# Two-chunk down products for both blocks of the paired FFN, with moved casts, moved sums of squares and an out-projection operand written by attention

## The chip, the cores and the metric

One core of a Trainium2 chip runs the kernel. The metric is the device time of one execution in microseconds (us). Below, PE is the matrix engine, DVE the vector engine, ACT the scalar engine, POOL GpSimd, and SP the engine whose queue issues nearly all DMAs. A *wait* is the time in which an engine's next instruction stands ready in its order but something that it needs is not done.

## The reference

All arrays are fp32: `x_sample` is 512 tokens, `x_prompt` 1024, of 1024 channels. Two layers run over both groups: layer 0 mixes tokens by a grouped Fourier transform, layer 1 by attention, and each is followed by a SwiGLU feed-forward network (FFN) with 2816 hidden channels.

```python
def attention_mixer(x, g, w_qkv, q_gain, k_gain, w_o, cos, sin):
    h = rms_norm(x, g)
    qkv = h @ w_qkv
    q, k, v = jnp.split(qkv, [Q_DIM, Q_DIM + KV_DIM], axis=-1)
    ...
    sc = jnp.einsum('bqkgd,bskd->bkgqs', qi, k).astype(jnp.float32) * scale
    p = jax.nn.softmax(sc, axis=-1).astype(v.dtype)
    return jnp.einsum('bkgqs,bskd->bqkgd', p, v)
    ...
    return o @ w_o

def swiglu_ffn(x, g, w_gate, w_up, w_down):
    h = rms_norm(x, g)
    return (jax.nn.silu(h @ w_gate) * (h @ w_up)) @ w_down

x = x + fourier_mixer(...) or attention_mixer(...)
x = x + swiglu_ffn(x, norm_ffn[i], ffn_w_gate[i], ffn_w_up[i], ffn_w_down[i])
```

There are 8 query heads and 2 key/value heads of 128, with RMS norm and rotary positions on queries and keys.

## The kernel before

**Tiles.** The tokens are three blocks of 512: block 0 is the sample, blocks 1 and 2 the prompt. Channels lie on the 128 partitions, so a block is 8 tiles of 128x512, and its residual lies in DRAM (`xres`). The hidden channels are 22 chunks of 128. Every product is made of three matmuls (`mm3`, lines 255 to 257): each operand is split into a high part in the matrix engine's format, which ACT casts (L248 for activations, L293 for weights), and a low part, the difference, which DVE or POOL subtracts (L249, L294).

**The single FFN** (`ffn`, block 0 of either layer) goes chunk by chunk: gate products `g` (24 matmuls), up products, SiLU, product, split into a `mid` tile, and then the down products `c`, 8 output tiles, which DVE adds to accumulators (L780). The down products of earlier chunks are put as items between later gate and up products (`one()`).

**The paired FFN** (`ffn_pair`, blocks 1 and 2) computes gate and up of two chunks for two blocks with seven matrix products in place of eight. Its steps are named by their moving operands, B11, B21, T2, T1, B22, T3, N4. Each step runs four j, 2 x 3 matmuls for each. The operands are sums and differences of the four normed quarters of the two blocks; `moving` computes them once per layer, writes them to DRAM, and `fetch` brings them back as pieces of 128x1024 fp32 into a ring of eight slots. In layer 1 some operands (`places`) stay in SBUF after their first load. A chunk's down weights are loaded and cast by `fetch_down`, called in the middle of B21 and T3. The down products of a block wait in the list `pend`, and `some()` takes from it between the ring matmuls. There are 11 iterations of two chunks.

**Order.** `weave` interleaves two generators by their stated costs, a main one (F) and a second (X); inside, each engine's instructions keep an order that the Tile scheduler chose, and each engine executes its own in order. The main stages in time: the sample's Fourier mixer (to about 195 us); the single FFN of layer 0 woven with the prompt's mixer and then `moving` (to about 540); pair 0, the paired FFN of layer 0, woven with block 0's attention (to about 1420); the single FFN of layer 1 woven with the prompt's projections, attention (1750 to 2150), out-projection and `moving` (to about 2340); pair 1, alone on PE, to the end.

**Around the change.** `new_residual` takes a block's output tiles one by one, stores them, and adds their squares (ACT L344, DVE L345); with the last one `rstd_cols` sums over the partitions by four small matmuls (L314) and runs a DVE chain. `attend` computes for each head and query tile the scores, their maximum (L1194), its product with the query's norm (L1195), the exponentials `p` (L1198), transposes, and the values; the output goes to DRAM (`dot`), and `reloaded` brings it back as the operand of the out-projection, for each block.

Of the kernel before, what the change touches and what calls it, by code (L numbers as in the profile page):

```python
# [17 lines left out]
P = 128  # L18
D = 1024
# [106 lines left out]
def trunk_kernel(ctx: ExitStack, tc: tile.TileContext, t: dict):  # L126
# [18 lines left out]
    for name, kw in (("sbH", {}), ("sbF", {}), ("sbX", {}), ("psF", PS), ("psX", PS)):  # L145
# [186 lines left out]
    def new_residual(b, dc, piece, out=None, stays=False, room=None):  # L332
# [6 lines left out]
        if dc == 0:  # L339
            ss[b] = room() if room else tl("ss", [TB], F32, "ss" + cur[0])  # L340
# [5 lines left out]
        if dc == NC - 1:  # L346
            rstd[b] = cp.tile([P, 4], F32, name=nm("rs"))
            rstd_cols(rstd[b], ss.pop(b), D)

    def normed(b, gain, got, ab, held=None):  # L350

        yield 2.0
# [404 lines left out]
    def ffn(layer, b, h, out=None):  # L757
# [52 lines left out]
        for fc in range(NF):  # L810
# [6 lines left out]
            for dc in range(NC):  # L817
# [5 lines left out]
                if not odd_ and dc >= 3:  # L823
                    one()
                if dc % 2:
                    yield 1.36 if odd_ or dc < 3 else 2.0 if dc == 3 else 2.7
# [3 lines left out]
            for dc in range(NC):  # L830
                if not odd_ and dc == 1:
                    want("gate", fc + 1)
                if dc == (2 if odd_ else 4):
                    want("up", fc + 1)
                if not (here and fc == 0):
                    part(wu, h, up, dc)
                if not odd_:
                    one(2 if dc == 3 else 1)
                elif dc >= 6:
                    one()  # L840
                if dc % 2:
                    yield 3.4 if not odd_ and dc == 3 else 2.7 if not odd_ or dc == 7 else 1.36
# [22 lines left out]
    def moving(blocks, gain, out, ring, helped):  # L865

        yield 2.0
        r = [in_rows(rstd[b]) for b in blocks]
        yield 1.0
        for j in range(4):  # L870
# [7 lines left out]
            for (d, k), x in v.items():  # L878
                dve.scalar_tensor_tensor(x, x, gain[:, 4 * d + j : 4 * d + j + 1], r[k], op0=ALU.mult, op1=ALU.mult)  # L879
# [19 lines left out]
            dve.tensor_tensor(v[0, 0], v[0, 1], v[0, 0], op=ALU.subtract)  # L899
            put("T1", v[0, 0])  # L900
# [3 lines left out]
            dve.tensor_tensor(v[1, 1], v[1, 1], v[0, 0], op=ALU.subtract)  # L904
# [3 lines left out]
            yield 5.0  # L908

    def ffn_pair(layer, blocks, ring, places, wide, outs):  # L910
# [5 lines left out]
        pieces, turns = [ring[:, n] for n in range(8)], [0]  # L916
        del order[:8]

        def fetch():
            if order:  # L920
                v, j = order.pop(0)
# [4 lines left out]
                else:  # L926
                    x = ring[:, turns[0] % 8]
                    turns[0] += 1
                sp.dma_start(x.bitcast(F32), mov[layer][v][:, j])
# [3 lines left out]
        first_raw = acc_tile("raw", [2, TB], F32)  # L933
        for b in blocks:
            accs[b] = kept[b] = accumulators()

# [4 lines left out]

        def down(b, parts, dc, begins, ends):
# [562 lines left out]
```

## Time and profile before

| quantity | value |
|---|---|
| median of three runs | 3043.49 us (3035.97 to 3046.52) |
| the profiled execution | 3038.65 us |
| its span | 3036.9 us |
| PE busy | 2925.5 us, 96% |
| POOL busy | 1338.7 us, 44% |
| DVE busy | 1487.2 us, 49% |
| DMA, mean | 180 GB/s |
| PE's granted clock, mean | 0.985 |

In the profile `L954` is a line of the kernel before; `acc<-c,acc` gives what is written and read, by the program's names without numbers; `x368` is a count. A view of windows gives, for a stretch of time, the busy time of each engine with its instructions, then the mean clock that PE was granted (PEclk, 1 is full), the share of the DMA engines' time and their rate. A PE busy share of 1 at a clock of 1 is the most that a stretch can do.

### The profile page before, as it was taken

What the parts mean: (1) busy time and instruction counts of PE and PEld (TensorE: products, weight loads), DVE (VectorE), ACT (ScalarE), POOL (GpSimd) and SP (SyncE); (2) the same over time, 40 slices, a digit from 0 to 9 for tenths busy, and PEclk for the clock granted to TensorE, in tenths of its full rate; (3) what the DMA queues carried; (4) which work ended last, traced back from release to release, by engine and by line L of the source; (5) the groups of instructions that cost most, each with busy time, mean ns of one, the idle gap of its engine ahead of it and who ended that gap; (6) DMA issues with size and microseconds to landing.
All of it is one profiled execution on the core that took longest, in us unless ns stands there. A gap on an engine that the chain in (4) does not pass through costs nothing. (4 is left out here: it accounts for less than half of the span.)

```text
span 3036.9 us, 37132 instructions
## 1 busy us (share of the span) xinstructions
PE 2925.5 (96%) x13920; PEld 2407.4 (79%) x13920; DVE 1487.2 (49%) x2537; ACT 1235.8 (41%) x1931; POOL 1338.7 (44%) x746
## 2 busy tenths in 40 slices
PE   7999989999999999999999999999998999999999
PEld 6888867778888788887778787788776788888887
DVE  6664663544436554336543456555335344444444
ACT  6543332333326664223444476777433222222221
POOL 4444345445444446542443322221546654555462
PEclk9999999999999999999999999999998999999999
DMA  7435474877767778865533211121657954445342
GB/s 228 153 118 174 167 259 134 289 273 241 248 228 250 238 232 290 298 229 191 187 121 102 90 60 59 60 67 46 207 178 256 332 194 154 139 153 198 134 139 90
DMA packets 204212, 547.15 MB, mean 180 GB/s; under 512 B 22304, under 2 KB 36640, under 8 KB 203648
## 3 DMA queue, kind: packets, MB, share of 16 engines
q1 hardware_dynamic: 203104, 539.99, 52.7%
q0 software_dynamic: 640, 3.74, 0.4%
q8 instruction: 109, 1.79, 0.2%
q10 hardware_dynamic: 288, 1.05, 0.1%
q14 instruction: 71, 0.58, 0.1%
HBM read 472.34 MB, written 72.35 MB: 179 GB/s over the span
## 5 line engine op out<-in xcount | busy, mean ns | idle before, releaser
L294 POOL TENSOR_TENSOR w<-raw,w 128x1024 fp32r<-128x1024 f32 x244 | 589.0, 2421 | 921.9 <-ACT w L293 898.3
L249 POOL TENSOR_TENSOR w<-raw,w 128x512 fp32r<-128x512 f32 (+1 forms) x332 | 436.9, 1337 | 620.1 <-ACT w L248 597.6
L954 DVE TENSOR_TENSOR acc<-c,acc 128x512 f32<-128x512 f32 x368 | 253.1, 689 | 410.7 <-PE c L257 402.9
L255 PE MATMUL c<-mid,w 128*128 128x512 f32 x1056 | 418.8, 397 | 20.5 <-ACT mid L248 9.0
L257 PE MATMUL c<-mid,w 128*128 128x512 f32 x1056 | 416.0, 394 | 4.0 <-POOL w L294 4.0
L256 PE MATMUL c<-mid,w 128*128 128x512 f32 x1056 | 416.2, 394 | 3.6 <-DVE mid L249 3.5
L293 ACT CAST w<-raw 128x1024 fp32r<-128x1024 f32 x244 | 254.9, 1049 | 319.0 <-PE c L257 111.4
L248 ACT CAST w<-raw 128x512 fp32r<-128x512 f32 (+1 forms) x332 | 197.2, 635 | 442.1 <-issue 185.7
L255 PE MATMUL g<-h,w 128*128 128x512 f32 x704 | 284.0, 403 | 7.6 <-ACT w L293 4.9
L257 PE MATMUL g<-h,w 128*128 128x512 f32 x704 | 281.7, 400 | 3.8 <-POOL w L294 3.8
L256 PE MATMUL g<-h,w 128*128 128x512 f32 x704 | 281.8, 400 | 0.0
L255 PEld LDWEIGHTS c<-mid,w 128*128 128x128 f32 x1056 | 199.9, 189 | 72.5 <-ACT mid L248 13.5
L257 PEld LDWEIGHTS c<-mid,w 128*128 128x128 f32 x1056 | 200.1, 190 | 47.4 <-POOL w L294 6.4
L256 PEld LDWEIGHTS c<-mid,w 128*128 128x128 f32 x1056 | 200.0, 189 | 47.4 <-DVE mid L249 7.7
L256 PE MATMUL c<-h,w 128*128 128x512 f32 x480 | 190.1, 396 | 7.7 <-POOL h L249 5.4
L255 PE MATMUL a<-ring,w 128*128 128x512 f32 x488 | 193.6, 397 | 3.5 <-DVE x L879 3.5
L257 PE MATMUL a<-ring,w 128*128 128x512 f32 x488 | 191.8, 393 | 3.0 <-POOL w L249 3.0
L255 PE MATMUL c<-h,w 128*128 128x512 f32 x480 | 190.5, 398 | 2.3 <-ACT h L248 1.4
L256 PE MATMUL a<-ring,w 128*128 128x512 f32 x488 | 191.7, 393 | 0.0
L257 PE MATMUL c<-h,w 128*128 128x512 f32 x480 | 188.3, 393 | 0.0
L780 DVE TENSOR_TENSOR acc<-c,acc 128x512 f32<-128x512 f32 x176 | 120.5, 687 | 130.8 <-PE c L257 128.5
L255 PEld LDWEIGHTS g<-h,w 128*128 128x128 f32 x704 | 135.9, 193 | 36.5 <-ACT w L293 6.0
(368 smaller groups left out, 5948.9 us busy)
## 6 DMA issues: line engine op xcount, KB each, us to landing
ring<-mov_B SPq DMA_DIRECT2D x204, 512.0 KB, 6.0
ring<-mov_T SPq DMA_DIRECT2D x176, 512.0 KB, 4.8
raw<-in_gate_dram SPq DMA_DIRECT2D x44, 512.0 KB, 3.6
raw<-in_up_dram SPq DMA_DIRECT2D x44, 512.0 KB, 3.6
raw<-in_down_dram SPq DMA_DIRECT2D x88, 256.0 KB, 3.1
raw<-in_gate_dram SPq DMA_DIRECT2D x88, 256.0 KB, 3.2
raw<-in_up_dram SPq DMA_DIRECT2D x88, 256.0 KB, 4.8
raw<-in_down_dram SPq DMA_DIRECT2D x44, 512.0 KB, 5.2
```

Source lines behind the costliest of these rows:

```text
L248: act.copy(hi, src)
L249: eng.tensor_tensor(lo, src, hi.bitcast(F32), op=ALU.subtract)
L255: pe.matmul(out, lh, rh, start=first, stop=False)
L256: pe.matmul(out, lh, rl, start=False, stop=False)
L257: pe.matmul(out, ll, rh, start=False, stop=last)
L293: pinned(act.copy(flat[:, 0], raw)) if early else act.copy(flat[:, 0], raw)
L294: pool.tensor_tensor(flat[:, 1], raw, flat[:, 0].bitcast(F32), op=ALU.subtract)
L780: dve.tensor_tensor(acc[dc], box[0], acc[dc], op=ALU.add)
L954: dve.tensor_tensor(acc, box[0], acc, op=ALU.add)
```

## The change

- *moving*: of the four normed quarters at every j, two are written to PSUM (`bank2`); the differences are ordered so that each reads one of them. The tiles of B22 and T3 get a pool of their own (three buffers). POOL makes the low parts of B21, T1, T3 and N4 in both layers; before, of B11 and B21 in layer 0, of B11, B21, B22, T3 and N4 in layer 1.
- *single FFN*: in the gate products the down items begin with weight tile 5 instead of 3, and three tiles of the up products take two items; the next gate weights are asked for two tiles later.
- *paired FFN*: the down products of both blocks are done after N4's beginning, two chunks at once for each (before, block 1's first chunk went alone in the first iteration, the last alone at the end). The products lie in four fixed slots, one of which is the eighth slot of the ring, so the ring of operands has seven. The down weights are loaded at the first j of T1 and of B22 and cast at the first j of B22 and T3. In layer 1 two quarters of gate and up weights are loaded one step earlier, in a pool of six.
- *end of pair 0*: the sums of squares get one tile a block, and the matmuls L314 with the chain behind them are made where the norm is first used (`settled`). The projections of layer 1 begin with block 2.
- *attention*: the maximum is taken bank by bank, and maximum and product are one instruction. For block 0, and for block 1 of the prompt, the values go straight into the operand of the out-projection (`straight`); for block 2 the way through DRAM stays.

```diff
 def normed(b, gain, got, ab, held=None):
+    settled(b)
 ...
 def ffn(layer, b, h, out=None):
-                if not odd_ and dc >= 3:
+                if not odd_ and dc >= 5:
                     one()
...
-                if not odd_ and dc == 1:
+                if not odd_ and dc == 3:
                     want("gate", fc + 1)
+                if fc == NF - 1 and dc == 4:
+                    want("B", f0)
...
-                    one(2 if dc == 3 else 1)
+                    one(2 if dc in (2, 4, 6) else 1)
 def moving(...):
+            a2 = bank2()
+            for (d, k), x in list(v.items()):
+                if d == k:
+                    v[d, k] = a2[:, d]
+                dve.scalar_tensor_tensor(v[d, k], x, gain[...], r[k], op0=ALU.mult, op1=ALU.mult)
...
+                elif name in ("B22", "T3"):
+                    x = tl("l", [2, TB], F32R, "mv", staging)
...
-            dve.tensor_tensor(v[0, 0], v[0, 1], v[0, 0], op=ALU.subtract)
-            put("T1", v[0, 0])
+            t1 = x4[:, 0, 0]
+            dve.tensor_tensor(t1, v[0, 1], v[0, 0], op=ALU.subtract)
+            put("T1", t1)
 def ffn_pair(...):
+        def load_down(fc):
+            coming[fc] = raw_tile(D)
+            sp.dma_start(coming[fc], t["down"][layer, fc])
+        def fetch_down(fc):
+            wds[fc] = w_tile(2, NC, P)
+            flat = wds[fc].rearrange("p h c n -> p h (c n)")
+            split(flat[:, 0], flat[:, 1], coming.pop(fc), eng=pool)
...
+        slots = [two[0], two[1], tl("mid", [2, TB], F32R, "m2", raws), ring[:, 7]]
+        where = {(0, 0): (0, 1), (0, 1): (1, 0), (1, 1): (2, 2), (1, 0): (3, 3)}
...
-            for i, ps in (yield from step("B21", lambda: fetch_down(f0), 2)):
+            for i, ps in (yield from step("B21")):
-            for i, ps in (yield from step("T2", lambda: downs(blocks[0], begins=f0 == 0), 2)):
+            for i, ps in (yield from step("T2")):
-            for i, ps in (yield from step("T1")):
+            for i, ps in (yield from step("T1", lambda: load_down(f0), 0)):
-            for i, ps in (yield from step("B22")):
+            for i, ps in (yield from step("B22", lambda: (fetch_down(f0), load_down(f1)), 0)):
-            for i, ps in (yield from step("T3", lambda: fetch_down(f1), 2)):
+            for i, ps in (yield from step("T3", lambda: fetch_down(f1), 0)):
-            for i, ps in (yield from step("N4", lambda: downs(blocks[1], begins=f0 == 0, ends=f0 + 2 == NF), 0)):
+            for i, ps in (yield from step("N4", lambda: downs(blocks[1], f0), 1)):
...
-        downs(blocks[0], ends=True)
+            downs(blocks[0], f0)
 def attend(blocks, straight, slot):
-                    dve.tensor_reduce(st[:, 0:1], s_in, op=ALU.max, axis=AX.X)
-                    dve.tensor_tensor(st[:, 1:2], st[:, 0:1], nrqc[:, gq, h : h + 1], op=ALU.mult)
+                    for kb in range(nb):
+                        dve.tensor_reduce(st[:, 2 * kb : 2 * kb + 1], sc[:, kb], op=ALU.max, axis=AX.X)
+                    dve.scalar_tensor_tensor(st[:, 1:2], st[:, 2 * nb - 2 : 2 * nb - 1], st[:, 0:1], nrqc[:, gq, h : h + 1], op0=ALU.max, op1=ALU.mult)
...
+                    if blocks[n] == straight:
+                        split(hs[:, 0, h, c0 : c0 + 256], hs[:, 1, h, c0 : c0 + 256], po[:, 0:256])
+                        return
 def aux_1():
-        yield from attend((0,))
+        yield from attend((0,), 0, "A")
 def aux_2():
-        for b in (1, 2):
+        for b in (2, 1):
             yield from qkv(b, kept[b])
-        yield from attend((1, 2))
+        yield from attend((1, 2), 1, "B")
```

Three places show what the scheduler makes of it. The first is DVE's order in the third of the four pieces of `moving` for pair 1 (`x` is the SBUF tile of the quarters, `l` a staged operand, `a` a PSUM tile, `acc<-c,acc` the single FFN's accumulations). Before:

```order
L899 TENSOR_TENSOR x_18456<-x_18456 128x512
L848 TENSOR_TENSOR g_18607<-g_18607,t_18703 128x512
L901 TENSOR_TENSOR x_18456<-x_18456 128x512
L249 TENSOR_TENSOR l_18495<-x_18456,l_18495 128x512
L904 TENSOR_TENSOR x_18456<-x_18456 128x512
L906 TENSOR_TENSOR x_18456<-x_18456 128x512
```

Now:

```order
L249 TENSOR_TENSOR ring_18121<-a_18332,ring_18121 128x512
L249 TENSOR_TENSOR l_18343<-a_18332,l_18343 128x512
L920 TENSOR_TENSOR x_18327<-x_18327,a_18332 128x512
L792 TENSOR_TENSOR acc_11448<-c_18699,acc_11448 128x512
L922 TENSOR_TENSOR x_18327<-a_18332,x_18327 128x512
L925 TENSOR_TENSOR a_18332<-a_18332,x_18327 128x512
```

The four differences (L899 to L906 before, L920 to L927 now) read `x` alone before and `x` and `a` now, and the accumulations of the single FFN stand between them.

The second is SP's order in the first iteration of pair 0 (`mov_B`, `mov_N`, `mov_T` are operands, `acc<-xres` the residual tiles that begin an accumulation). Before:

```order
L929 DMA ring_3281<-mov_B_103 128x1024 x4
L929 DMA ring_3281<-mov_T_104 128x1024
L951 DMA acc_4040<-xres_95 128x512
L929 DMA ring_3281<-mov_T_104 128x1024
L951 DMA acc_4040<-xres_95 128x512
L929 DMA ring_3281<-mov_T_104 128x1024
L982 DMA raw_4942<-in_gate_dram 128x512
```

Now:

```order
L965 DMA ring_3281<-mov_B_103 128x1024 x4
L965 DMA ring_3281<-mov_T_104 128x1024 x4
L965 DMA ring_3281<-mov_N_105 128x1024 x4
L965 DMA ring_3281<-mov_B_99 128x1024 x4
L965 DMA ring_3281<-mov_B_100 128x1024 x3
```

The residual tiles leave this stretch, and the operands of five steps follow each other.

The third is DVE's order where block 2's last column ends pair 0 (`sq` and `ss` hold squares and their sums, L302 to L308 are the chain of `rstd`). Before:

```order
L954 TENSOR_TENSOR acc_4042<-c_11443,acc_4042 128x512
L345 TENSOR_TENSOR sq_11360<-sq_11440,sq_11360 128x512
L345 TENSOR_TENSOR sq_11360<-sq_11452,sq_11360 128x512
L302 TENSOR_SCALAR c_11456<-c_11456 128x4
L303 TENSOR_SCALAR c_11456<-c_11456 128x4
L304 TENSOR_SCALAR col_11461<-c_11456 128x4
L954 TENSOR_TENSOR acc_4039<-c_11474,acc_4039 128x512
```

Now:

```order
L1011 TENSOR_TENSOR acc_4054<-c_11325,acc_4054 128x512
L345 TENSOR_TENSOR ss_11248<-sq_11322,ss_11248 128x512
L345 TENSOR_TENSOR ss_11248<-sq_11334,ss_11248 128x512
L1011 TENSOR_TENSOR acc_4051<-c_11338,acc_4051 128x512
L1011 TENSOR_TENSOR acc_4051<-c_11342,acc_4051 128x512
L345 TENSOR_TENSOR ss_11350<-sq_11358,ss_11350 128x512
```

The chain of `rstd` no longer stands between the columns of the two blocks.

More of the change, by code (lines that the diff above doesn't have):

```diff
@@ L330, in accumulators, with new_residual @@
         return [a[:, i] for a in halves for i in range(4)]
-    def new_residual(b, dc, piece, out=None, stays=False, room=None):
+    def new_residual(b, dc, piece, out=None, stays=False, room=None, later=None):
         if out is not None:
@@ L915, in ffn_pair, with taken @@
         order = [(v, j) for n in range(NF // 2) for v in OPERANDS if n == 0 or v not in places for j in range(4)]
-        pieces, turns = [ring[:, n] for n in range(8)], [0]
+        pieces, turns, full, owed = [ring[:, n] for n in range(8)], [0], [7], [0]
+        held_ = [True] * 7 + [False]
         del order[:8]
-        def fetch():
-            if order:
-                v, j = order.pop(0)
+        def taken():
+            x = pieces.pop(0)
+            full[0] -= held_.pop(0)
+            owed[0] += 1
+            return x
+        def fetch():
+            while owed[0] and order:
+                v, j = order[0]
+                if v not in places and full[0] == 7:
+                    break
+                del order[0]
+                owed[0] -= 1
                 if v in places:
@@ L926, in fetch @@
                 else:
-                    x = ring[:, turns[0] % 8]
+                    x = ring[:, turns[0] % 7]
                     turns[0] += 1
+                    full[0] += 1
+                held_.append(v not in places)
                 sp.dma_start(x.bitcast(F32), mov[layer][v][:, j])
@@ L955, in half, with downs @@
                     if ends:
-                        new_residual(b, dc, acc, None if outs is None else outs[b][:, dc, :], room=spare)
+                        new_residual(b, dc, acc, None if outs is None else outs[b][:, dc, :], room=spare, later=sums_of(b, dc))
             return [lambda k=k: half(k) for k in range(len(parts))]
-        mids, nmid = {b: [] for b in blocks}, [2]
-        def downs(b, begins=False, ends=False):
+        mids = {b: [] for b in blocks}
+        two = [tl("mid", [2, TB], F32R, "mid") for _ in range(2)]
+        slots = [two[0], two[1], tl("mid", [2, TB], F32R, "m2", raws), ring[:, 7]]
+        open_ = [0] * 4
+        where = {(0, 0): (0, 1), (0, 1): (1, 0), (1, 1): (2, 2), (1, 0): (3, 3)}
+        def downs(b, f0):
             parts, mids[b] = mids[b], []
-            lists = [down(b, parts, dc, begins, ends) for dc in range(NC)]
+            lists = [down(b, parts, dc, f0 == 0, f0 + 2 == NF) for dc in range(NC)]
             for k in range(len(parts)):
@@ L1013, in times, with hidden @@
             return list(enumerate(banks))
-        def hidden(up, s, b, wd):
+        def hidden(up, s, fc, k):
             dve.tensor_tensor(up, up, s, op=ALU.mult)
-            nmid[0] += 1
-            m = tl("mid", [2, TB], F32R, "mid") if nmid[0] % 3 else tl("mid", [2, TB], F32R, "m2", raws)
+            n = where[fc % 2, k][fc // 2 % 2]
+            assert not open_[n], (fc, k)
+            open_[n] = NC
+            m = slots[n]
             split(m[:, 0], m[:, 1], up)
-            mids[b].append((m, wd))
+            mids[blocks[k]].append((n, fc))
         def silu(s, x):
@@ L1336, in aux_0, with paired @@
         close_pool("mp")
[L1337 to L1339 removed]
+        yield from paired(0, {}, False, None)
+    def paired(layer, places, wide, outs):
         ring = h_slot("ring", F32R, "B")[:, 0 : 16 * TB].rearrange("p (s h n) -> p s h n", s=8, h=2)
[L1342 removed]
+        yield from moving((1, 2), g_ffn[layer], mov[layer], ring, ("B21", "T1", "T3", "N4"))
         close_pool("sbX")
@@ L1380, in aux_2 @@
         close_pool("ap")
-        yield from paired(1, ("B11", "B21", "B22", "T3", "N4"), {"T1": here, "B22": here, "T3": late, "N4": late}, True, t["y"])
+        yield from paired(1, {"T1": here, "B22": here, "T3": late, "N4": late}, True, t["y"])
     late_ = []
```

71 lines of the change are left out of this document (46 added, 25 removed), and 2 rows, old and new, of the table BUFS.

## The prediction

> **What bounds the kernel now.** I read the page first: which engine is full.
>
> ```profile
> PE 2925.5 (96%) x13920; PEld 2407.4 (79%) x13920; DVE 1487.2 (49%) x2537; ACT 1235.8 (41%) x1931; POOL 1338.7 (44%) x746
> ```
>
> TensorE (PE) is busy for 96% of a span of 3036.9 us, and the change leaves its work alone. What can be won is the 111 us in which it stands still, and the time in which it runs at a lowered clock. The windows, by stage, show where both are (window, length, busy us of each engine, PEclk, DMA share, GB/s).
>
> ```profile
> 385.00:455.00 70.00, 60.60 (x236) 47.30 (x235) 45.38 (x57) 23.38 (x33) 33.64 (x16) 0.90 0.76 257
> 540.00:660.00 120.00, 112.57 (x483) 89.43 (x484) 62.57 (x102) 39.27 (x67) 54.33 (x34) 0.97 0.84 296
> 660.00:1400.00 740.00, 730.06 (x3393) 602.67 (x3392) 334.85 (x580) 294.09 (x491) 356.90 (x219) 1.00 0.75 252
> 1400.00:1460.00 60.00, 50.06 (x208) 40.25 (x207) 49.58 (x81) 28.04 (x43) 18.47 (x8) 0.91 0.49 175
> 1750.00:2150.00 400.00, 386.32 (x2249) 324.31 (x2247) 222.82 (x363) 288.95 (x411) 90.92 (x38) 1.00 0.20 64
> 2150.00:2240.00 90.00, 84.28 (x349) 66.11 (x350) 19.30 (x37) 30.39 (x44) 53.34 (x30) 0.96 0.67 214
> 2240.00:2345.00 105.00, 89.28 (x358) 70.44 (x357) 60.87 (x77) 36.96 (x58) 51.44 (x30) 0.89 0.63 228
> 2345.00:2450.00 105.00, 101.23 (x440) 81.79 (x440) 41.09 (x61) 27.57 (x45) 64.12 (x38) 1.00 0.87 314
> 2450.00:3000.00 550.00, 550.00 (x2426) 454.72 (x2426) 234.14 (x348) 139.91 (x236) 291.18 (x182) 1.00 0.43 147
> ```
>
> From 2450 to 3000 PE never stops: 550/2426 = 0.227 us a matmul, the floor. The dear places are the seams, where one stage hands to the next: 385–455 and 2240–2345 (`moving` writes the pairs' operands while the single FFN still runs), 540–660 (pair 0 begins) and 1400–1460 (pair 0 ends). I count loss as length less busy, plus (1 − clock) × busy: 9.4 + 6.1 = 15.5 us; 7.4 + 3.4 = 10.8; 9.9 + 4.5 = 14.4; 15.7 + 9.8 = 25.5. Attention (1750–2150) loses 13.7, and 2150–2240 5.7 + 3.4 = 9.1. What PE waits for, from the view of waits (us in total, times, longest):
>
> ```profile
> PE a L255 <- ACT p L1198: 9.3, 8, 2.0
> PE c L255 <- ACT mid L248: 9.0, 6, 4.2
> PE c L314 <- DVE sq L345: 6.3, 2, 3.7
> PE c L256 <- POOL h L249: 5.4, 8, 1.8
> PE g L255 <- ACT w L293: 4.9, 2, 4.0
> PE c L257 <- POOL w L294: 4.0, 5, 1.2
> PE a L255 <- DVE x L879: 3.5, 1, 3.5
> PE c L255 <- ACT w L293: 2.8, 2, 1.7
> ```
>
> Behind several of these lies one mechanism. In the timeline at the end of pair 0 (start, length, engine, line):
>
> ```profile
> 1426.89 5.14 POOL L294 TENSOR_TENSOR w<-raw,w 128x1024 fp32r<-128x1024 f32 x2 [13.90 <-ACT w L293]
> 1427.37 5.21 DVE L345 TENSOR_TENSOR sq<-sq,sq 128x512 f32<-128x512 f32 x2 [0.24 <-ACT sq L344]
> 1432.63 1.53 PE L314 MATMUL c<-ones,sq 128*128 128x1 f32 x8 [3.74 <-DVE sq L345]
> ```
>
> Two DVE additions take 5.2 us, exactly beside two POOL instructions of 5.1, and PE waits for them. The groups by form say which DVE operations are so held (busy us, mean ns, after the count):
>
> ```profile
> L954 DVE TENSOR_TENSOR acc<-c,acc 128x512 f32<-128x512 f32 x368 | 253.1, 689 | 410.7 <-PE c L257 402.9 <-DMA acc<-xres 7.1
> L1194 DVE TENSOR_REDUCE col<-a 128x1 f32<-128x1024 f32 x64 | 78.4, 1224 | 116.0 <-PE a L257 116.0
> L1195 DVE TENSOR_TENSOR col<-col,nrqc 128x1 f32<-128x1 f32 x96 | 51.4, 536 | 1.5
> L249 DVE TENSOR_TENSOR l<-x,l 128x512 fp32r<-128x512 f32 x28 | 26.9, 973 | 2.6 <-ACT l L248 2.6
> L1194 DVE TENSOR_REDUCE col<-c 128x1 f32<-128x512 f32 x32 | 22.1, 690 | 22.1 <-PE c L257 21.9
> L345 DVE TENSOR_TENSOR sq<-sq,sq 128x512 f32<-128x512 f32 x14 | 16.6, 1183 | 0.5 <-ACT sq L344 0.4
> L904 DVE TENSOR_TENSOR x<-x 128x512 f32<-128x512 f32 x8 | 11.8, 1472 | 0.2
> ```
>
> With one input in PSUM (`c`) the mean is 689 ns; with both in SBUF it is 973 to 1472, as they stand until POOL's instruction ends.
>
> **The change, part by part.** *Moving.* At every j, two of the four normed pieces now go to PSUM, so each of the four differences and every split reads one operand there. Four differences of about 1.4 us and their splits come to 0.69 us each: about 4 us off DVE per piece, on a chain of which this is one link:
>
> ```profile
> 432.98 2.92 POOL L294 TENSOR_TENSOR w<-raw,w 128x1024 fp32r<-128x1024 f32 x1 [2.24 <-ACT w L293]
> 434.22 2.23 DVE L906 TENSOR_TENSOR x<-x 128x512 f32<-128x512 f32 x1
> ```
>
> It ended at 436.4; the gate's product and its split stood behind it in DVE's order, and PE then waited 4.2 us for the mid (the longest of `ACT mid L248`). In layer 0 POOL gets splits of three operands more and loses one: 8 more over the four pieces, at 1337 ns,
>
> ```profile
> L294 POOL TENSOR_TENSOR w<-raw,w 128x1024 fp32r<-128x1024 f32 x244 | 589.0, 2421 | 921.9 <-ACT w L293 898.3
> L249 POOL TENSOR_TENSOR w<-raw,w 128x512 fp32r<-128x512 f32 (+1 forms) x332 | 436.9, 1337 | 620.1 <-ACT w L248 597.6
> ```
>
> so 10.7 us more in a stretch in which POOL worked 33.6 of 70: hidden. With the single FFN's downs begun two weight tiles later, I keep a third of the loss: **−10** of 15.5 (bounds −5, −14). In layer 1 the seam reads, on PE:
>
> ```profile
> 2309.24 0.50 PE L255 MATMUL g<-h,w 128*128 128x512 f32 x1 [4.04 <-ACT w L293]
> 2312.12 0.79 PE L257 MATMUL g<-h,w 128*128 128x512 f32 x1 [2.15 <-POOL w L294]
> 2327.32 0.76 PE L255 MATMUL a<-ring,w 128*128 128x512 f32 x1 [3.50 <-DVE x L879]
> ```
>
> Casts of the gate's weights stand behind operand splits on ACT and POOL; the last wait also holds a whole chunk of `g` matmuls queued behind it, which the new order puts ahead of the pair's first matmul. **−18** of 25.5 (−8, −23); what is late next is the first weights of pair 1 (345 to 2450 loses only 3.8 in its 105).
>
> *Attention.* The maximum over 1024 scores (1224 ns) becomes two over 512 (690 each), the first under the matmuls of the second bank: 1224 − 690 = 0.53 us off the chain of each of the 8 waits for `p`, **−4** (0, −6). The fused multiply that follows still has both inputs in SBUF and is held as L1195 was, so the rest of the 9.3 stays. Block 1's heads go straight into the out-projection's operand; its reload, whose splits are half of the waits for `POOL h L249` (5.4), falls away: I take **−4** of the 9.1 (−1, −6), since block 2 is reloaded as before. The straight split puts 32 subtractions of about 0.4 us on DVE, which is idle for 177 of these 400 us.
>
> *End of pair 0.* The `rstd` matmuls and their chain leave PE's path (6.3 us of waits), but both blocks' last columns now run almost unbroken: 16 columns of 6 matmuls, 1.36 us each, against 0.69 for the accumulation and 0.69 for the sum of squares, which still reads SBUF twice. POOL's 2421-ns casts hold those; two or three such meetings cost 2.42 − 0.69 = 1.7 us each. **−7** of 14.4 (0, −11).
>
> *The pairs.* Eight accumulations fewer per layer are 5.5 us of a DVE with 50% to spare: nothing. Down weights are cast one or two steps ahead of their use; the waits for them at 595–640 (4.0 and 2.8, nearly all there) and their share of the clock: **−5** (−2, −7). Against it stands that until the seventh step of the first iteration no down product runs at all, and the ring holds seven operands, not eight. The DMA side:
>
> ```profile
> ring<-mov_B SPq DMA_DIRECT2D x204, 512.0 KB, 6.0
> 590.00:600.00 10.00, 7.84 (x38) 5.99 (x37) 1.50 (x4) 3.74 (x7) 4.30 (x3) 1.00 1.02 403
> 2390.00:2400.00 10.00, 10.00 (x46) 8.29 (x45) 5.34 (x8) 1.14 (x2) 3.02 (x3) 1.00 1.02 404
> ```
>
> A piece of 524 KB at 404 GB/s is 1.30 us; PE spends 6 × 0.227 = 1.36 on it. The first iteration uses 28 pieces, 38.1 us; to be brought in are 20 of them, four pairs of weight quarters and two down tiles, 26 × 1.30 = 33.8. The 4.3 us left must take the last residual stores (8 × 262 KB, 5.2 us): short by 1; with as many residual reads for the other stage, by 6. Before, 24 down matmuls (5.4 us) lay in this stretch as cover. Idle time cost another half of itself in clock in the windows above (3.4 beside 7.4, 4.5 beside 9.9). **+4** in pair 0 (1 to 9), **+3** in pair 1, whose stages share the DMA with less (0 to 7).
>
> Sum: −10 − 18 − 4 − 4 − 7 − 5 + 7 = −41, from the profiled execution's 3038.65 to 2998. That execution lies 4.8 below the median; half of this is put back: 3000 for the median of new runs, 41 below 3041.
>
> **A rule against the trace.** After one stall of 2.2 us the matmuls grow from 0.50 to 0.63, in a window with a clock of 0.90:
>
> ```profile
> 390.46 0.50 PE L255 MATMUL g<-h,w 128*128 128x512 f32 x1 [2.19 <-ACT t L847]
> 392.35 0.63 PE L256 MATMUL g<-h,w 128*128 128x512 f32 x1
> ```
>
> The Trainium skill (TensorE: Matmul & The Clock Gate, HAM oscillation) has the clock fall for idle gaps above about 3.4 us. By that rule most stalls here, 2 to 3 us long, would cost no clock, and the gain would be the idle parts of the terms alone, about 32 of 48 us, an estimate by that rule. The row speaks against it: 2.2 us of idleness were enough, and the sum keeps the clock.
>
> **The rivals.** (1) *The operands starve the first iterations.* For it: DMA at 1.02 with nothing to spare. Against: the ring begins full. With both upper ends (9 + 7) the cost is 16 instead of 7: 3009. (2) *DVE stays held.* The sums of squares and the products before PSUM still read SBUF twice; if the seams keep their stalls, moving gives 13 rather than 28 (its lower bounds) and pair 0's end nothing: 3000 + 15 + 7 = 3022. (3) *Slower: POOL late in every iteration.* The two down casts, 2.42 us each, now stand at the head of two neighbouring steps (B22, T3), ahead of the stationary weights of the next one; before they stood in the middle of steps four apart. If one cast's length is not covered, PE stalls 2.42 in each of 2 × 11 iterations: 53 us, so 3053. From 41/22 = 1.9 us an iteration the gain is gone. Against: POOL works 291 of 550 us in pair 1, and PE has waited for nothing there. (4) *Stalls of 2 to 3 us cost no clock*, so that their removal returns the idle parts alone: at the ratios of idle to loss in the windows (9.4 of 15.5, 15.7 of 25.5, 9.9 of 14.4, 7.4 of 10.8, and attention's whole) −32 instead of −48, so 3016. Against it stands the row at 392. (5) *The order the scheduler gives hides little of what the edit wins*: the stalls move to the next late tile and the time stays within 0.3% (9 us, about what a measurement of this kernel can tell from no change): 3040.
>
> **How the numbers follow.** My forecast 0.5, the first rival 0.12, the second 0.13, the third 0.1, the fourth 0.05, the fifth 0.1. Own range of the forecast, with the bounds of the terms partly offsetting: 2980 to 3016. The range that leaves no more than 2 in 10 out reaches over the second and fourth to 3032, and down to 2978. Faster by over 0.3% are the forecast and rivals 1, 2 and 4: 0.8; within 0.3% the fifth: 0.1; slower the third: 0.1.
>
> **What would show it.** Right: moving's differences at about 0.69 us; windows at 385–455 and about 2200–2310 with a clock of 0.95 and more; no PE wait for L314; the reductions at 690; no reload of block 1. Wrong: waits of ring matmuls for DMA in either pair's first iteration (rival 1), sums of squares near 2 us and PE waits on accumulations at pair 0's end (2), an idle of some 2 us before the first matmul of T3 or N4 in each of the eleven iterations (3).

## The result, and the profile after

The changed kernel takes 2997.66 us (median of four runs, 2985.28 to 2997.93), the kernel before beside it 3044.83; the ratio is 0.9841, 95% interval 0.9809 to 0.9873. The forecast was 3000. The profiled execution took 2997.49 us, 41.2 less than the 3038.65 of before; the sum of the prediction's terms was −41. That the two agree so closely is partly luck, as the stages show: three terms failed, in both directions, and some 5 us of the changed kernel's profiled time lie in its start, where the code is nearly unchanged.

The page of the changed kernel, engines first:

```profile
span 2995.7 us, 36963 instructions
PE 2905.0 (97%) x13920; PEld 2404.5 (80%) x13920; DVE 1473.7 (49%) x2613; ACT 1224.9 (41%) x1911; POOL 1317.6 (44%) x734
```

PE does the same 13920 matmuls. It stands still for 90.7 us instead of 111.4, which is 20.7 us of the gain; the other 20.5 lie in its busy time, 2905.0 instead of 2925.5. The clock accounts for about 9 of these: its mean is 0.988 where it was 0.985, so (1 − clock) × busy goes from 43.9 to 34.9 us. What shortened the rest of the busy time is not shown. The same windows as before the change (window, length, busy us of PE, its loads, DVE, ACT, POOL, then PEclk, DMA share, GB/s):

```profile
385.00:455.00 70.00, 67.39 (x287) 54.46 (x286) 39.65 (x61) 27.43 (x40) 43.48 (x26) 0.98 0.83 287
540.00:660.00 120.00, 115.85 (x511) 94.48 (x510) 64.85 (x99) 41.62 (x70) 56.54 (x34) 0.97 0.88 306
1750.00:2150.00 400.00, 382.97 (x2218) 324.33 (x2218) 227.93 (x419) 279.24 (x397) 95.89 (x41) 0.99 0.20 64
2150.00:2240.00 90.00, 87.90 (x391) 71.61 (x390) 25.05 (x55) 29.50 (x45) 38.22 (x21) 0.98 0.58 187
2240.00:2345.00 105.00, 92.34 (x391) 73.90 (x390) 51.29 (x78) 38.70 (x63) 65.82 (x40) 0.95 0.81 286
2345.00:2450.00 105.00, 104.90 (x462) 86.21 (x462) 42.35 (x65) 26.86 (x45) 59.46 (x37) 1.00 0.80 291
```

Around the end of pair 0 the work is arranged anew, so for that seam and for what follows it wider windows are compared, the first two of the kernel before, the last two of the changed one:

```profile
1300.00:1480.00 180.00, 169.40 (x739) 138.13 (x738) 104.12 (x170) 63.57 (x100) 74.44 (x39) 0.97 0.63 215
1460.00:1750.00 290.00, 280.93 (x1327) 228.00 (x1326) 122.19 (x246) 124.40 (x178) 111.88 (x47) 0.98 0.38 117
```

```profile
1300.00:1480.00 180.00, 170.98 (x756) 137.38 (x755) 107.65 (x162) 69.81 (x107) 81.64 (x42) 0.99 0.66 231
1460.00:1750.00 290.00, 285.30 (x1389) 233.82 (x1388) 125.42 (x271) 128.97 (x185) 104.92 (x44) 0.99 0.33 104
```

Loss, as in the prediction, is length less busy, plus (1 − clock) × busy. The clock is printed to two digits, so a long window is uncertain by some 2 us. The first 100 us differ between executions by more than 5 us: the 448th matmul, which comes in the same order in every kernel here, ends at 95.3 us in the run gate1 below, at 95.4 in the kernel before, at 100.4 in the changed kernel and at 101.0 in the run old_max, with a mean clock in these 100 us of 0.93, 0.93, 0.86 and 0.85. So the profiled pair understates the change by about 5 us.

| stage | loss before | after | change | predicted |
|---|---|---|---|---|
| start (0–100) | 25.5 | 31.0 | +5.5 | 0 |
| moving, layer 0 (385–455) | 15.5 | 4.0 | −11.5 | −10 |
| pair 0 begins (540–660) | 10.8 | 7.6 | −3.2 | −5 + 4 |
| end of pair 0 (1300–1480) | 15.7 | 10.7 | −5.0 | −7 |
| projections (1460–1750) | 14.7 | 7.6 | −7.1 | 0 |
| attention (1750–2150) | 13.7 | 20.9 (17.0 idle) | +7 | −4 |
| out-projection (2150–2240) | 9.1 | 3.9 | −5.2 | −4 |
| moving, layer 1 (2240–2345) | 25.5 | 17.3 | −8.2 | −18 |
| pair 1 begins (2345–2450) | 3.8 | 0.1 | −3.7 | +3 |

Two rows share 1460 to 1480 and the stretches between are left out, so the rows do not add up to the 41.2 us. What PE waits for now, the groups on which the text rests:

```profile
PE a L255 <- ACT p L1264: 11.7, 10, 1.8
PE c L323 <- ACT t L322: 8.3, 4, 4.7
PE g L255 <- ACT w L293: 7.4, 1, 7.4
PE c L255 <- DVE acc L1011: 5.5, 5, 2.6
PE c L255 <- ACT mid L248: 3.5, 3, 1.9
PE a L255 <- DMA ring<-mov_N: 0.2, 1, 0.2
```

The waits for `mid` fell from 9.0 to 3.5, those for the norm's sums (L314) at the end of pair 0 from 6.3 to none. But the row that is made from the norm (L323) is waited for longer, 8.3 us where it was 4.6, and 2.7 of these stand at the end of pair 0. Operands from DMA are waited for in one place, 0.2 us. The waits on accumulations (L1011, 5.5) lie at 1335 to 1359, all but 0.2. The waits for `p` in attention rose from 9.3 to 11.7, and a single one of 7.4 us stands at the seam before pair 1.

### The profile page after: what moved, and what is told of

Read it like the earlier page. It is cut to its first block, busy times and chain, and to the rows that moved or that the text cites. A ratio compares the mean times of both kernels' runs of the same rounds, so it can differ in the third digit from the quotient of the medians.

```text
span 2995.7 us, 36963 instructions
## 1 busy us (share of the span) xinstructions
PE 2905.0 (97%) x13920; PEld 2404.5 (80%) x13920; DVE 1473.7 (49%) x2613; ACT 1224.9 (41%) x1911; POOL 1317.6 (44%) x734
## 5 line engine op out<-in xcount | busy, mean ns | idle before, releaser
L249 POOL TENSOR_TENSOR w<-raw,w 128x512 fp32r<-128x512 f32 (+1 forms) x376 | 542.5, 1467 | 673.1 <-ACT w L248 671.4
L294 POOL TENSOR_TENSOR w<-raw,w 128x1024 fp32r<-128x1024 f32 x200 | 479.1, 2403 | 815.8 <-ACT w L293 810.0
L248 ACT CAST w<-raw 128x512 fp32r<-128x512 f32 (+1 forms) x376 | 242.8, 684 | 495.5 <-PE a L257 171.1
L1011 DVE TENSOR_TENSOR acc<-c,acc 128x512 f32<-128x512 f32 x352 | 241.7, 689 | 355.5 <-PE c L257 346.0
L255 PE MATMUL c<-mid,w 128*128 128x512 f32 x880 | 347.6, 395 | 12.8 <-DVE acc L1011 5.5
L257 PE MATMUL c<-mid,w 128*128 128x512 f32 x880 | 344.8, 392 | 2.2 <-POOL w L294 2.2
L256 PE MATMUL c<-mid,w 128*128 128x512 f32 x880 | 345.0, 392 | 1.4 <-DVE mid L249 1.3
L293 ACT CAST w<-raw 128x1024 fp32r<-128x1024 f32 x200 | 208.7, 1049 | 286.4 <-PE g L257 79.9
L255 PE MATMUL g<-h,w 128*128 128x512 f32 x704 | 280.6, 399 | 9.8 <-ACT w L293 7.4
L257 PE MATMUL g<-h,w 128*128 128x512 f32 x704 | 278.8, 396 | 3.9 <-POOL w L294 3.9
L256 PE MATMUL g<-h,w 128*128 128x512 f32 x704 | 279.2, 397 | 0.0
L255 PEld LDWEIGHTS c<-mid,w 128*128 128x128 f32 x880 | 166.0, 189 | 55.3 <-DVE acc L1011 11.5
L257 PEld LDWEIGHTS c<-mid,w 128*128 128x128 f32 x880 | 165.7, 188 | 38.0 <-POOL w L294 3.5
L256 PEld LDWEIGHTS c<-mid,w 128*128 128x128 f32 x880 | 166.0, 189 | 36.6 <-DVE mid L249 3.1
L792 DVE TENSOR_TENSOR acc<-c,acc 128x512 f32<-128x512 f32 x176 | 120.4, 687 | 124.0 <-PE c L257 122.8
```

The costliest lines, as they stand in the source:

```text
L248: act.copy(hi, src)
L249: eng.tensor_tensor(lo, src, hi.bitcast(F32), op=ALU.subtract)
L255: pe.matmul(out, lh, rh, start=first, stop=False)
L256: pe.matmul(out, lh, rl, start=False, stop=False)
L257: pe.matmul(out, ll, rh, start=False, stop=last)
L293: pinned(act.copy(flat[:, 0], raw)) if early else act.copy(flat[:, 0], raw)
```

## The experiments

All start from the changed kernel; times are medians of four runs. One kernel's runs spread over 1.5 us (ring5) to 17 us (old_max), the changed kernel's own from 2985 to 2998. Of the intervals of the ratio to the kernel before, only those of m_sbuf, early_max and old_pair lie clear of the changed kernel's (0.9809 to 0.9873). For the others the times alone settle nothing, and the traces are read.

**The normed quarters in SBUF.**

```diff
-            a2 = bank2()
...
                 if d == k:
-                    v[d, k] = a2[:, d]
+                    v[d, k] = x
```

> The changed kernel, but moving writes all four normed quarters to SBUF; POOL's splits, the staging pool and the rest stay. Theory (DVE with two SBUF inputs stands still while POOL works): the differences and the operand splits rise from 0.69 us to a mean of 1.1 to 1.5, the two seams (about 385-455 and 2240-2345) lose 8 to 16 us more together, and the time is 3005 to 3015. Rival (the seams gained by the later downs and POOL's other splits, the place of the data is indifferent): within 4 us of the changed kernel's 2997.5.

3006.25 us, ratio to before 0.9901 (0.9881 to 0.9920): 8.6 slower than the changed kernel. In the groups by form the differences and splits (line numbers one lower than in the changed kernel) are:

```profile
L249 DVE TENSOR_TENSOR l<-x,l 128x512 fp32r<-128x512 f32 x16 | 21.6, 1353 | 0.4 <-ACT l L248 0.4
L919 DVE TENSOR_TENSOR x<-x 128x512 f32<-128x512 f32 x8 | 12.4, 1549 | 0.0
L926 DVE TENSOR_TENSOR x<-x 128x512 f32<-128x512 f32 x8 | 11.3, 1408 | 0.4
```

and in the changed kernel

```profile
L249 DVE TENSOR_TENSOR l<-a,l 128x512 fp32r<-128x512 f32 x16 | 11.0, 688 | 5.7 <-ACT l L248 5.5
L922 DVE TENSOR_TENSOR x<-a,x 128x512 f32<-128x512 f32 x8 | 5.5, 683 | 0.1
L927 DVE TENSOR_TENSOR x<-x,a 128x512 f32<-128x512 f32 x8 | 5.4, 678 | 0.0
```

The four differences, of which two are shown, take 678 to 690 ns on average with one operand in PSUM and 1280 to 1549 with both in SBUF. PE's wait of the kernel before returns almost to the digit, in a timeline of PE, where the changed kernel has 0.66 us at its place:

```profile
440.14 0.80 PE L255 MATMUL c<-mid,w 128*128 128x512 f32 x1 [4.07 <-ACT mid L248]
```

So the hold is the cause in layer 0. The window 385–540 shows 144.44 busy at a clock of 0.97 against 149.15 at 0.99, a loss of 14.9 against 7.3 (16.8 in the kernel before): most of the gain there goes back with this line. At the other seam the undone line makes little difference (89.20 busy at 0.97 against 92.34 at 0.95, 18.5 against 17.3): moving in layer 1 is bound by something else, below.

**One maximum as before; two maxima issued earlier; and the product freed.** Three kernels on attention's chain.

```diff
# old_max: as before
-                    for kb in range(nb):
-                        dve.tensor_reduce(st[:, 2 * kb : 2 * kb + 1], sc[:, kb], op=ALU.max, axis=AX.X)
-                    dve.scalar_tensor_tensor(st[:, 1:2], ..., op0=ALU.max, op1=ALU.mult)
+                    dve.tensor_reduce(st[:, 0:1], s_in, op=ALU.max, axis=AX.X)
+                    dve.tensor_tensor(st[:, 1:2], st[:, 0:1], nrqc[:, gq, h : h + 1], op=ALU.mult)
# early_max: each maximum right behind its score product
                     for kb in range(nb):
                         mm3(sc[:, kb], ...)
+                        dve.tensor_reduce(st[:, 2 * kb : 2 * kb + 1], sc[:, kb], op=ALU.max, axis=AX.X)
...
-                    for kb in range(nb):
-                        dve.tensor_reduce(st[:, 2 * kb : 2 * kb + 1], sc[:, kb], op=ALU.max, axis=AX.X)
# early_ts: early_max, and
-                    dve.scalar_tensor_tensor(st[:, 1:2], st[:, 2 * nb - 2 : 2 * nb - 1], st[:, 0:1], nrqc[...], ...)
+                    dve.tensor_scalar(st[:, 1:2], st[:, 2 * nb - 2 : 2 * nb - 1], st[:, 0:1], nrqc[...], ...)
```

> The changed kernel with one maximum over 1024 and a separate product, as before. The prediction's term: 4 us slower, since 0.53 us comes back at each of eight waits. Theory from the trace of the changed kernel (both halves start only after the last score matmul, 1.29 us for the two against 1.22 for the one): no change, within 3 us, apart from what a new order brings.

> The changed kernel, with the first half's maximum issued between the two score products. If the first half waited only because it was issued behind both products, it now starts about 0.7 us before the last score matmul ends; the product of maximum and norm then starts 0.6 us earlier, often ahead of POOL's cast (which began 0.2 us before it in the stalls seen): waits for p fall from 11.7 to 4-8 us, time 2990 to 2995. Rival: the two halves still start together (the tile is waited for as a whole): waits for p stay at 11 to 12, time within 3 us of 2997.5.

> As early_max, and the product takes the second maximum and the norm as per-partition scalars, so that only one input is an SBUF tensor. Theory (the hold needs two SBUF tensor inputs): no such instruction over 0.3 us, where 2.3 us was the longest; waits for p 2 to 5 us, time 2987 to 2993. Rival (any DVE instruction that reads only SBUF is held by POOL): the longest stays near 2.3 us and the time is that of early_max.

old_max: 2999.84 us (ratio 0.9861, 0.9837 to 0.9885), no difference; its waits for `p` are 12.3 in place of 11.7. The reason stands in a timeline of the changed kernel, where the two products of one score tile end and the maxima begin:

```profile
1782.48 0.39 PE L257 MATMUL a<-w,w 128*128 128x512 f32 x1
1783.16 0.39 PE L257 MATMUL a<-w,w 128*128 128x512 f32 x1
1783.59 1.29 DVE L1260 TENSOR_REDUCE col<-a 128x1 f32<-128x512 f32 x2 [0.54 <-PE a L257]
1785.39 0.21 DVE L1261 SCALAR_TENSOR_TENSOR col<-col,nrqc 128x1 f32<-128x1 f32 x1
```

The first bank was complete at 1782.9, yet DVE, idle for 0.54 us, starts on it at 1783.6, after the second bank's last matmul. Two maxima then take 1.29 us, where one took 1.22. Nothing was hidden.

early_max: 3022.15 us (0.9942, 0.9927 to 0.9957), 24 slower, which neither theory expected. Its timeline:

```profile
1855.88 0.68 DVE L1257 TENSOR_REDUCE col<-a 128x1 f32<-128x512 f32 x1
1856.62 0.19 PEld L255 LDWEIGHTS a<-w,w 128*128 128x128 f32 x1 [0.18 <-DVE col L1257]
1857.62 0.69 DVE L1257 TENSOR_REDUCE col<-a 128x1 f32<-128x512 f32 x1
```

Now the first maximum starts early, and the second score product waits for it: the write of bank 1 stands behind the read of bank 0. The two-bank tile is ordered as a whole in both directions. The 24 us are lost elsewhere, though. In attention's window PE is busy for 387.54 of 400, more than the changed kernel's 382.97; the loss comes later, where PE waits in one piece:

```profile
PE a L255 <- DVE x L927: 22.3, 1, 22.3
PE g L255 <- ACT w L248: 8.5, 1, 8.5
```

In PE's order of instructions, 315 matmul rows of `mm3` in the changed kernel lie between the last out-projection matmul and the first of pair 1; here there are 220, since the scheduler put the attention and the out-projection behind more of the single FFN. The single FFN's last gate or up matmul ends at 2301, pair 1 begins at 2339, and `moving` has only down products as cover. From the end of the last out-projection matmul to the first matmul of pair 1 pass 78.1 us here, 80.1 in early_ts, 83.5 in ts_max and 88.7 in the changed kernel: with fewer matmuls in between, more of this time is waiting. This is read from the traces; no run changes the order alone.

early_ts: 3004.89 us (0.9887, 0.9872 to 0.9902). The product's longest case falls from 2356 ns to 277, and in attention's window the waits for `p` are gone (398.07 busy of 400). But the seam takes 13.7 and 8.6 us of waits, for the same reason: 247 rows as cover. So the theory on the hold stood, and the expected time of 2987 to 2993 did not come, for want of that cover.

**The freed product alone.** The changed kernel with only the last of the edits above, the maxima left where they were.

> The changed kernel with its two maxima where they are, and the product of maximum and norm made with the second maximum and the norm as per-partition scalars (one SBUF tensor input). Theory (the hold by POOL is what PE waits for in attention; the earlier runs lost at the next seam because PE's order there left moving fewer matmuls as cover, 220 and 247 rows against 315): here 299 rows are left, attention (1750-2150) loses 10 us less, the seam 2 to 4 us more, time 2986 to 2993. Rival (a shorter chain in attention is always given back at the seam): 2998 or more.

2983.03 us (2977.85 to 2986.37), ratio 0.9814 (0.9789 to 0.9838), 14.6 less than the changed kernel. Attention's window and the seam:

```profile
1750.00:2150.00 400.00, 399.98 (x2301) 339.78 (x2300) 210.61 (x421) 283.62 (x402) 105.60 (x45) 1.00 0.23 75
2240.00:2345.00 105.00, 87.19 (x347) 68.78 (x346) 41.34 (x64) 30.55 (x49) 56.43 (x35) 0.90 0.83 301
```

PE stands still for 0.02 us in 400. The two groups, the changed kernel's ahead (mean 569 ns over all 96, 206 at best) and this one's behind:

```profile
L1261 DVE SCALAR_TENSOR_TENSOR col<-col,nrqc 128x1 f32<-128x1 f32 x96 | 54.5, 569 | 1.4
```

```profile
L1261 DVE TENSOR_SCALAR col<-col,nrqc 128x1 f32<-128x1 f32 x96 | 25.7, 269 | 1.3
```

A result of one element for each partition had cost up to 2356 ns, and the exponentials of the tile wait for it. In the changed kernel's trace 24 of the 96 took over 700 ns, and each of them ended within 0.03 us of the end of a POOL instruction. As per-partition scalars the two other inputs are not held, though they lie in SBUF like the first: the longest of the 96 takes 281 ns. The Trainium skill (GPSIMD Engine Reference, Specifications) has the SBUF interfaces shared between GpSimd and VectorE, with contention for VectorE instructions that have two SBUF inputs. The trace agrees with it: up to 2356 ns with two such inputs, at most 281 with one. At the seam 9 us more are lost than in the changed kernel (17.8 idle and 8.7 of clock, against 12.7 and 4.6), where 2 to 4 were expected: a part of attention's gain is given back there.

**The sums of squares at once, and the whole paired FFN of before.**

```diff
# sums_now
-  new_residual(b, dc, acc, ..., room=spare, later=sums_of(b, dc))
+  new_residual(b, dc, acc, ..., room=spare)
# old_pair: ffn_pair is that of the kernel before, all of it
```

> The changed kernel with the sums of squares and the norm's chain made at once when each block's last column is done, as before. Prediction: its term of 7 us comes back, 3004, with waits of PE for L314 near 6 us in 1340-1460. Rival (the gain at pair 0's end came from the even run of two-chunk columns, not from the moved chain): within 3 us of 2997.5.

> The changed kernel with the paired FFN of before: down products of one or two chunks, ring of eight, casts in the middle of B21 and T3, sums and chain at once. Prediction: the waits for down weights at 590-640 return (+5) and the end of pair 0 is as before (+7), but 7 us for operands that come late are won back: 3003. Theory from the changed kernel's trace (only 0.2 us of waits for operands, so there is nothing to win back): 3010. Rival (all of the gain lies in moving and the single FFN): 2998.

sums_now: 2999.99 us (0.9871, 0.9839 to 0.9904). The wait for L314 returns once (3.7 us, where before there were two), and 1300–1480 loses 14.6 instead of 10.7; in the time 2.3 us are not to be told from nothing. old_pair: 3015.26 us (0.9918, 0.9893 to 0.9942), 17.6 slower than the changed kernel, more than either theory said and the largest of the single parts. Its end of pair 0:

```profile
1300.00:1480.00 180.00, 162.85 (x699) 131.88 (x698) 109.72 (x171) 61.65 (x99) 73.01 (x41) 0.95 0.66 226
PE c L314 <- DVE sq L345: 5.7, 2, 3.9
PE c L256 <- DVE mid L249: 5.2, 1, 5.2
PE c L255 <- DVE acc L976: 3.9, 3, 1.6
```

It loses 25.3 there, 14.6 more than the changed kernel. Four of these are the moved chain (sums_now). The rest is left, by subtraction, to what else the paired FFN changed; that it is the even row of two-chunk down products, in place of single chunks behind a fresh `mid`, is likely (the wait of 5.2 us for a `mid`) but not tried alone.

**Two operands less ahead.**

```diff
-                if v not in places and full[0] == 7:
+                if v not in places and full[0] >= 5:
...
-                    x = ring[:, turns[0] % 7]
+                    x = ring[:, turns[0] % 5]
```

> The changed kernel with at most five operands ahead instead of seven. Theory of rival 1 (operands starve the first iterations, each piece less costs 1.36 us of cover): waits of PE for operands from DMA in the first iteration of both pairs, 3 to 10 us in all, and 3003 to 3015. From the changed kernel's 0.2 us of such waits: still under 1 us, time within 4 us of 2997.5, since the median slack was over ten us.

3002.44 us (0.9867, 0.9845 to 0.9890), 4.8 slower. Waits for operands appear at once:

```profile
PE g L255 <- DMA ring<-mov_T: 5.4, 3, 3.0
PE g L255 <- DMA ring<-mov_N: 4.1, 2, 3.5
PE a L255 <- DMA ring<-mov_T: 3.9, 3, 1.9
PE a L255 <- DMA ring<-mov_N: 1.6, 2, 0.9
```

They come to 15.2 us with a last group of 0.2, but only 3.1 of them in the first iteration (540–660); the others are spread over pair 0 to 1400, and none lies in pair 1. So neither expectation held, the one on the place and the other on the size. Seven slots were enough, five are not.

**The gate weights asked for earlier; the single FFN of before; the reload for every block.**

```diff
# gate1
-                if not odd_ and dc == 3:
+                if not odd_ and dc == 1:
                     want("gate", fc + 1)
# old_single: ffn is that of the kernel before, all of it
# reload
-                    if blocks[n] == straight:
+                    if False and blocks[n] == straight:
```

> The changed kernel, but the single FFN asks for its next gate weights at the second weight tile of the up products again, not at the fourth. Theory (the 7.4-us wait at 2304 is a gate load issued on SP behind moving's stores and loads at 2297 and landed 6.4 us later): the load is issued 0.9 us or more earlier and in part ahead of those; the wait falls to 2 to 5 us, time 2990 to 2996. Rival (SP's queue is held by moving's stores at that place whatever the order): the wait stays at 6 to 8 us and the time within 3 us of 2997.5.

> The changed kernel with the single FFN of before (downs from the fourth weight tile on, the gate weights asked for at the second). If the later downs carry part of the gain at the two seams, mid waits return near 385-455 and 2240-2345: +3 to +8, 3001 to 3005. Since the run gate1 showed 11 us for the earlier gate weights alone, the rival is: faster than the changed kernel, 2985 to 2995, the earlier weights being worth more than the later downs.

> The changed kernel, but attention writes all blocks' outputs to DRAM and each out-projection reads its operand back, as before. Prediction: its term of 4 us comes back, 3002, with PE waits for the first splits of block 1 after about 2150. Rival (the reload is hidden behind other work, or its stall only moves into slack): within 3 us of 2997.5.

gate1: 2986.74 us (0.9829, 0.9805 to 0.9854), a median 10.9 lower, but not by the wait it was aimed at, which is still 6.99 us (7.43 in the changed kernel). On SP's queue the gate load stands behind moving's stores and loads with either setting; in the changed kernel, from the timeline of SP, with PE's wait:

```profile
2289.79 2.34 SPq L913 DMA_DIRECT2D mov_T<-l  x3
2294.80 2.25 SPq L891 DMA_DIRECT2D x<-xres  x4
2297.09 0.43 SPq L289 DMA_DIRECT2D raw<-in_gate_dram  x1
2304.68 0.79 PE L255 MATMUL g<-h,w 128*128 128x512 f32 x1 [7.43 <-ACT w L293]
```

The rival was right about the wait. The lower time comes from earlier places. The profiled execution is 9.4 us lower; 5.1 of these lie in the start, where nothing was changed, and the rest at 385–540, which is 152.56 us busy at a clock of 1.00, a loss of 2.4 against 7.3. So some 4 us, not 10.9, can be put down to the edit.

old_single: 2991.56 us (0.9831, 0.9807 to 0.9854), 6 faster than the changed kernel. It includes the earlier gate weights, and the later downs gain nothing that shows. At the second seam the change of the single FFN even costs:

```profile
2288.19 0.33 SPq L289 DMA_DIRECT2D raw<-in_gate_dram  x1
2292.68 2.06 SPq L911 DMA_DIRECT2D mov_T<-l  x3
2240.00:2345.00 105.00, 99.22 (x427) 79.78 (x426) 53.31 (x81) 41.37 (x68) 68.53 (x42) 0.98 0.83 297
```

With the single FFN of before the same gate load goes ahead of moving's stores of `mov_T`, lands after 4.3 us instead of 6.4, and PE does not wait for it; the window loses 7.8 instead of 17.3, and the one before it (2150–2240) 6.2 instead of 3.9.

reload: 2994.22 us (0.9843, 0.9819 to 0.9868), no slower. Its waits for the splits of `h` are 4.7 us against 2.1, and the window 2150–2240 loses 3.1 against 3.9. Writing the operand directly saves no time here.

**Both edits that gained.** The freed product and the earlier gate weights together.

> Both edits that made the changed kernel faster: the product with per-partition scalars (-14.6) and the earlier gate weights (-10.9). If they act at different places (attention; 400-450 and 540-660) and neither is run-to-run spread, the sum: 2972 to 2976. If the second is spread, or both meet at the seam before pair 1: 2980 to 2986.

2980.27 us (2975.08 to 2983.58), ratio 0.9797 (0.9770 to 0.9825): the fastest of all, 17.4 below the changed kernel and 63 below the kernel before beside it. Its lead over ts_max, 2.8, lies inside the spread; the sum of the two, 2972 to 2976, did not come. The seam has become the dearest place:

```profile
2240.00:2345.00 105.00, 87.03 (x341) 68.51 (x340) 40.96 (x63) 29.35 (x48) 54.50 (x35) 0.89 0.84 302
```

## Why the prediction was right, and where it was not

**Moving, layer 0: right**, in mechanism and size. −11.5 against −10, and one line undone brings the old wait back. That the later downs of the single FFN share in it was wrong: with the FFN of before the window loses 3.0, not more than the 4.0 here.

**Moving, layer 1: the mechanism holds, the term was mis-sized.** −18 stood for −8.2 here and −3.7 in the window behind (the bounds were −8 and −23). The wait of 3.5 us for `x` is gone, and the pair's first matmul no longer blocks `g` matmuls. But what was named as late next, pair 1's first weights, was not it: a gate load of the single FFN, landing 6.4 us after an issue behind moving's stores, costs 7.4. The prediction counted a wait for gate weights (4.04 us) among what is won; the run old_single shows that the new order of the single FFN's items keeps one of these waits, since with the old order the load goes ahead and the window loses 7.8. Asking for the weights earlier (gate1) is not enough.

**Attention: wrong.** The step that failed is "the first under the matmuls of the second bank". The two halves run after the second bank. That the product stays held was right, and ts_max showed that it was all of the loss there: waits of 10.5 us for `p` in that window become none. The prediction named this hold and did not see its worth. That the loss rose by 7 is no cost of the split maximum: with the same attention code the window loses 12.1 us in old_pair and 15.3 in sums_now, so it goes with the order. The 32 subtractions that the prediction put on DVE here are 16 for block 1, of which the window shows 14 of 422 ns.

**Out-projection: the size right, the reason wrong.** The window lost 5.2 us less, 4 was forecast; but with the reload put back it loses no more. The order of the new kernel covers these splits with or without the reload.

**End of pair 0: about right** (−5 for −7), but the step "the `rstd` matmuls and their chain leave PE's path" carries only some 4 of it, and the cost set against it did not come. From the timelines of DVE and PE in the changed kernel:

```profile
1343.40 2.89 DVE L252 SCALAR_TENSOR_TENSOR h<-t,gains,h 128x512 fp32r<-128x512 f32 x1
1350.20 4.51 DVE L379 TENSOR_TENSOR t<-r,t 128x512 f32<-128x512 f32 x2
1423.33 0.69 DVE L1011 TENSOR_TENSOR acc<-c,acc 128x512 f32<-128x512 f32 x1
1424.26 5.27 DVE L345 TENSOR_TENSOR ss<-sq,ss 128x512 f32<-128x512 f32 x2 [0.24 <-ACT sq L344]
1442.80 0.49 PE L323 MATMUL c<-t,ones 128*128 128x128 f32 x2 [2.69 <-ACT t L322]
```

The last sums are held for 5.27 us as feared, but after the last accumulation, when no column waits behind them; PE goes through the 16 columns from 1401 to 1424 with one wait of 0.24 us. The chain has not quite left PE's path: behind it PE waits 2.69 us for the row made from the norm (L323), so of the 6.3 us some 3.6 are gone. What PE does wait for is earlier, at 1335 to 1359: accumulations that stand on DVE behind the norm of block 0 (L252, L379), whose inputs both lie in SBUF and which is held beside POOL's instructions (2.89 us where the shortest of L252 there is 0.74). In the kernel before 1300 to 1360 lost nothing, and the same norm ran from 1399 to 1417, in the seam itself. So "DVE stays held" came true at a place that the prediction did not look at.

**The pairs: the cover was undervalued.** The waits for down weights at 595 to 640 are gone, as said; waits for block 0's norm (4.1 us, 1.1 before) took part of their place, and with the paired FFN of before the window loses 9.5, only 1.9 more. The terms +4 and +3 for late operands were wrong: 0.2 us. The count of pieces was right as a warning only, since with two slots less 15 us of such waits appear.

**Not foreseen:** the projections after pair 0 lose 7 us less. Neither the moved sums nor the paired or single FFN of before nor the reload bring this loss back (sums_now loses 7.5 in that window, old_pair 8.4, old_single 7.5, reload 7.4, the changed kernel 7.6). The order in which blocks 2 and 1 are projected is the likeliest that is left, and it was not tried alone.

**The rivals.** Starved first iterations and POOL late in every iteration did not come: PE stood still for 0.1 us between 2345 and 2450, the start of pair 1. DVE still held came true for attention and the norm of block 0. That stalls of 2 to 3 us cost no clock did not come either. In the kernel before, right behind the stall of 2.19 us that ended at 390.46, the granted clock is at half:

```profile
392.00:395.40 3.40, 3.40 (x9) 1.95 (x7) 0.69 (x1) 1.53 (x2) 3.07 (x2) 0.50 0.84 279
```

Its trace has 15 such drops to half after the first 100 us, of 3.4, 6.8 or 10.2 us, but only four stalls longer than 3.4 us (4.2, 4.0, 3.7 and 3.5). The Trainium skill (TensorE: Matmul & The Clock Gate, HAM oscillation) counts idle gaps above about 3.4 us. The trace does not agree with that, and the measurement decides: shorter stalls cost clock too.

**The parts do not add up.** Undone one by one, they give, in medians of which only the first two are clear of the spread, 8.6 (PSUM in moving), 17.6 (paired FFN), 2.2 (maxima), −3.4 (operand) and −6.1 (single FFN), 19 in all of the 47 us between the medians. The rest lies in parts not undone alone (POOL's choice of splits, the staging pool, the order of projections) or in the order, which changes with every edit. Which, stays open.

## What to carry to other kernels

Look at the longest case of a group, not the mean: a DVE operation on one element that sometimes takes 2.3 us has an operand pattern that another engine can hold, and here a change of form (per-partition scalars, or an operand in PSUM) frees it (as scalars the shortest case grows from 206 to 261 ns). Where a scheduler sets the order, a shorter chain can make the kernel slower by moving the cover away from the next seam, so count the matmuls that lie between the last input and the first use before trusting a gain. And before splitting an operation to start its first half early, look whether the first half's start moves; a tile may be waited for as a whole.

## What the runs showed of the hardware

A DVE instruction of one element with two SBUF tensor inputs took from 206 to 2356 ns, the long ones until a POOL instruction of 1.3 or 2.4 us ended; the same with pointers as scalars took 261 to 281 ns, beside POOL's instructions too. A subtraction of 128x512 takes 680 ns with one input in PSUM beside POOL, 1280 to 1549 on average with both in SBUF. And right behind a stall of 2.19 us PE's clock stood at half for 3.4 us; over the whole change 20.7 us less of idle time came with about 9 us less lost to the clock, and with 11 us less of busy time that the clock does not account for.
